# Low halves of split weights: by an accumulating DMA from GpSimd in place of a VectorE subtraction

## The chip, the cores and the metric

The kernel runs on one core of a Trainium2 chip, as one program in one launch. The metric is the device time of the whole program in microseconds (us). PE is TensorE, DVE VectorE, ACT ScalarE, POOL GpSimd, and SP is SyncE, which only issues DMAs here.

## The reference

One inference step of a two-layer encoder for two groups of tokens that share weights: 512 prompt positions and 32 later ones, 544 columns in all. For each layer, all in float32:

```
z = x @ w_in                                  # columns for three branches
A = chunked gMLP gating;  B = latent attention (8 heads);  C = RG-LRU
x = LN(ALPHA * x + concat(A, B, C) @ w_o)     # 1024 x 1024
up = x @ ffn_w_up                             # 1024 x 5632
f = gelu(conv3(up)[:, :2816]) * conv3(up)[:, 2816:]
x = LN(ALPHA * x + f @ ffn_w_down)            # 2816 x 1024
```

The outputs are x of both groups and a set of caches and states.

## The kernel before

Activations lie transposed, features on the 128 partitions and the 544 columns in the free dimension, in two halves of 272. To get more than the precision of one pass, each float32 operand a is split into a high part, rounded to the type float32r, and a low part a - high, also float32r. A product of two operands is then three matmuls (`mm3`, lines 89 to 91): high by high, high weight by low x, low weight by high x. TensorE runs nothing but such triples in the projections.

A weight tile is 128 partitions by up to 8 blocks of 128 columns (512 KB, or 448 KB with 7 blocks). `load_w` has SyncE load it into one of 4 raw buffers (`wr`). `split_w` takes a high and a low buffer (`wh`, `wl`, five of each, in rotation) and calls `split`: ScalarE copies the raw tile to the high part (line 64), VectorE subtracts the high part from the raw tile (line 67). `page_weights` does the same with two half tiles in general pages, for weights that are prepared well ahead of their stage. `gate` holds two instructions behind which the planner has to put the splits.

The order on each engine is made by a planner. It goes by program order as a priority, but moves what is ready in its own model ahead of what is not. Each engine then runs its queue strictly in order and waits by semaphores.

The stages of a layer that concern the change:

- `wo_stage`: eight tiles of w_o by `proj_ln`, with the sums for the LayerNorm between them. It also prepares the first five tiles of the up projection (`pre_up`: two in wh/wl buffers, three in pages).
- `ffn`: the 22 pairs (gate g and value v) of the up projection in three blocks of 7, 7 and 8, each followed by its share of the down projection (8 tiles of 7, 7 and 8 blocks; `proj` twice, `proj_ln` in the end). A plain tile (`up_w`) is 16 triples for each half. The pairs 8, 10, ..., 20 are mixed pairs instead: `forms` makes seven combinations of weights, `seven` multiplies them with combinations of x (A11, A12, then S2, S1, S3, then S4, A22), and its three parts run between the halves of the plain pair that follows:

```
fa, fb, fc, fd = pair(8), pair(8), pair(8), pair(4)   # four of the five wh and wl buffers
...
w = up_w(l, *tl)
for hv in range(2):
    ev(tl, hv, mms([w], KU, hv)[0])
    if mix is not None and next(mix, True):
```

- `ev` lets ScalarE copy a half out of PSUM into a page `xp`, whose first two columns GpSimd sets to zero (`begin`, line 1086), and `post` lets VectorE do the convolution.
- `pre_in` prepares three tiles of the next layer's w_in, two of them by `page_weights`.

The weights of the mixed pairs, of the mixers (`col_weights`, `weights`) and of w_in tile 0 keep the VectorE subtraction.

Of the kernel before, what the change touches and what calls it, by code (L numbers as in the profile page):

```python
# [8 lines left out]
F32R = mybir.dt.float32r  # L9
AF = mybir.ActivationFunctionType  # L10
ALU = mybir.AluOpType
# [13 lines left out]
NI = 22  # L25
# [21 lines left out]
def trunk_kernel(ctx: ExitStack, tc: tile.TileContext, i, o, k):  # L47
    nc = tc.nc
    pool = ctx.enter_context(tc.tile_pool(name="sb", bufs=1))
    psum = ctx.enter_context(tc.tile_pool(name="ps", bufs=1, space=bass.MemoryType.PSUM))  # L50
    dram = ctx.enter_context(tc.tile_pool(name="dr", bufs=1, space=bass.MemoryType.DRAM))
    BUFS = dict(pg=28, pt=12, kb=8, pp=6, wr=4, wh=5, wl=5)

    def page(name, dt=F32, tag="pg"):
        return pool.tile([128, W if tag == "pp" else PG], dt, tag=tag, name=name, bufs=BUFS[tag])
# [7 lines left out]
    def act(out, in_, func=AF.Copy, **kw):  # L63
        return nc.scalar.activation(out=out, in_=in_, func=func, **kw)  # L64

    def tt(out, a, b, op, e=None):
        return (e or nc.vector).tensor_tensor(out=out, in0=a, in1=b, op=op)  # L67

    def stt(out, a, s, b, op0, op1):
        return nc.vector.scalar_tensor_tensor(out=out, in0=a, scalar=s, in1=b, op0=op0, op1=op1)  # L70
# [7 lines left out]
    def split(hi, lo, src, e=None):  # L78
        act(hi, src)
        tt(lo, src, hi.bitcast(F32), ALU.subtract, e)  # L80
# [12 lines left out]
    gate = []  # L93
    def load_w(src, kk, cols, name):
        wr = pool.tile([128, kk, cols], F32, tag="wr", name=name + "r", bufs=BUFS["wr"])
        nc.sync.dma_start(out=wr, in_=src)
        return wr
# [4 lines left out]
    def split_w(wr, kk, cols, name):  # L102
        wh = pool.tile([128, kk, cols], F32R, tag="wh", name=name + "h", bufs=BUFS["wh"])
        wl = pool.tile([128, kk, cols], F32R, tag="wl", name=name + "l", bufs=BUFS["wl"])
        with ExitStack() as st:
            for ins in gate:
                st.enter_context(tc.issue_after(ins.ins))
            split(wh, wl, wr)
        return wh, wl

    def weights(src, kk, cols, name):
        return split_w(load_w(src, kk, cols, name), kk, cols, name)

    def rsqrt(y, v, t):
        a = act(y, v, AF.Abs_reciprocal_sqrt)
        tt(t, y, y, ALU.mult)
        stt(t, t, -0.5, v, ALU.mult, ALU.mult)
        return a, stt(y, t, 1.5, y, ALU.add, ALU.mult)
# [84 lines left out]
    def col_weights(src, kk, name, kper=8):  # L203
        res = []
        for c in range(0, kk, kper):
            n = min(kper, kk - c)
            wh, wl = weights(src[:, 128 * c:128 * (c + n)].rearrange("p (k c) -> p k c", k=n), n, 128, name)
            for j in range(n):
                res.append((wh, wl, j))
        return res  # L210

    def page_weights(src, name, tag="pg"):
        wr = load_w(src.rearrange("p (k c) -> p k c", k=8), 8, 128, name)
        res = []
        for c in (0, 4):
            h, lo = page(name + "h", F32R, tag), page(name + "l", F32R, tag)
            h, lo = (t[:, 0:512].rearrange("p (k c) -> p k c", k=4) for t in (h, lo))
            with ExitStack() as st:
                for ins in gate:
                    st.enter_context(tc.issue_after(ins.ins))  # L220
                split(h, lo, wr[:, c:c + 4, :])
            res += [(h, lo, j) for j in range(4)]
        return res

    def mms(ws, kts, hv, hook=None, at=2):
        bs = [bank("mm") for _ in ws]
        nk = len(kts)
        for j in range(nk):
            for b, w in zip(bs, ws):
                wh, wl, ci = w[j]  # L230
                rh, rl = kts[j]
                mm3(b[:, 0:HW], wh[:, ci, :], wl[:, ci, :], rh[:, HV[hv]], rl[:, HV[hv]], j == 0, j == nk - 1)
            if hook is not None and j == at:
                hook()
        return [b[:, 0:HW] for b in bs]
# [707 lines left out]
            if self.spill is not None:  # L943
                nc.sync.dma_start(out=self.spill[m], in_=x)

    def proj(wsrc, kts, evac, name, kper):
        for ms in ((0, 1), (2,), (3,), (4,), (5,), (6,), (7,)):
            ws = [col_weights(wsrc(m), len(kts), f"{name}{m}", kper) for m in ms]
            for hv in range(2):
                for m, ps in zip(ms, mms(ws, kts, hv)):  # L950
                    evac(m, hv, ps)

    def proj_ln(wsrc, kts, ln, name, kper, ns, pre, mid, ko=None):
        n1 = 8 - ns

        def get(m):
            w = col_weights(wsrc(m), len(kts), f"{name}{m}", kper)
            return [w[j] for j in ko] if ko else w

        for ms in ((0, 1), (2,), (3,)):  # L960
            ws = [get(m) for m in ms]
            for hv in range(2):
                for m, ps in zip(ms, mms(ws, kts, hv)):
                    ln.evac(m, hv, ps)
            if ms[0] == 0 and mid is not None:
                mid()
        w = get(4)
        for hv in range(2):
            ps = mms([w], kts, hv)[0]
            ln.shift(hv)  # L970
            ln.evac(4, hv, ps)
        for m in range(5, n1):
            w = get(m)
            for hv in range(2):
                ln.evac(m, hv, mms([w], kts, hv)[0])
        ln.warm()
        ws = [get(m) for m in range(n1, 8)]
        nxt = pre() if pre is not None else None
        for j in range(ns):
            ln.evac(n1 + j, 0, mms([ws[j]], kts, 0)[0])  # L980
        for j in range(ns):
            ps = mms([ws[j]], kts, 1, (lambda: ln.stats(0)) if j == 0 else None, 5)[0]
            if j == 0 and not ln.final:
                ln.apply(0, range(4))
            ln.evac(n1 + j, 1, ps)
        if ln.final:
            ln.stats(1)
            ln.apply(0)
        else:
            ln.apply(0, range(4, 8))  # L990

        def hook():
            if not ln.final:
                ln.stats(1)
            ln.apply(1)
        rest = [] if ln.final else [lambda m=m: ln.settle(m) for m in range(8)]
        return nxt, hook, rest

    def wo_stage(l, va, pre):
        xT = []  # L1000
        for m in range(8):
            x = page(f"xT{m}")
            nc.sync.dma_start(out=x[:, 0:W], in_=xd[l][m])
            if m >= 4:
                act(x[:, 0:W], x[:, 0:W], scale=ALPHA)
            xT.append(x)
        ln = LN(xT, "alpha", va, C_LN1G, C_LN1B, None, False)
        ko = [6, 7, 2, 3, 0, 4, 1, 5]

        kts = [KX[m] for m in ko]  # L1010
        return xT, *proj_ln(lambda m: i["wo"][l, m], kts, ln, "wo", 8, 3, pre, None, ko)

    def up_w(l, i_, s):
        return col_weights(i["wup"][l, NI * s + i_], 8, "wup", 8)

    def pre_up(l):
        return [up_w(l, j // 2, j % 2) if j < 2 else page_weights(i["wup"][l, NI * (j % 2) + j // 2], "wup") for j in range(5)]
# [45 lines left out]
    def ffn(l, va, vf, xT, first, hook, rest, pre):  # L1063
# [13 lines left out]
        for bl, (i0, nk) in enumerate(BLK):  # L1077
            fts = []
# [84 lines left out]
            for tl in tiles[done:]:  # L1163
# [6 lines left out]
                w = up_w(l, *tl)  # L1170
# [5 lines left out]
            def wsrc(m):  # L1176
                return i["wdn"][l, m, :, 128 * i0:128 * (i0 + nk)]

            if bl < len(BLK) - 1:
                def ev2(m, hv, ps):  # L1180
                    x = xT[m][:, HV[hv]]
                    if bl == 0:
                        stt(x, x, ALPHA, ps, ALU.mult, ALU.add)
                    else:
                        tt(x, x, ps, ALU.add)
                proj(wsrc, fts, ev2, "wd", 8)
            else:
                fin = l == DEPTH - 1

                def mid():  # L1190
                    nc.sync.dma_start(out=o[7][l], in_=fo)

                ln = LN(xT, "add", va, C_LN2G, C_LN2B, o[0] if fin else xd[l + 1], fin)
                nxt = proj_ln(wsrc, fts, ln, "wd", 8, 2, pre, mid)
        return nxt

    def pre_in(l):
        res = []
        for m in range(3):
            w = col_weights if m == 0 else page_weights  # L1200
            res.append(w(i["win"][l, m], 8, f"win{m}") if m == 0 else w(i["win"][l, m], f"win{m}"))
        return res

    vecs = {}
    nxt, hook = load_x()
    rest = []
    for l in range(DEPTH):
        mixer(l, nxt, hook, rest)
        va, vf, kvg, sp4 = vecs[l]
        xT, nxt, hook, rest = wo_stage(l, va, lambda: pre_up(l))  # L1210
        nxt, hook, rest = ffn(l, va, vf, xT, nxt, hook, rest, (lambda: pre_in(l + 1)) if l + 1 < DEPTH else None)
# [119 lines left out]
```

## Time and profile before

| | |
|---|---|
| median of 3 runs | 1272.6 us (1271.58 to 1275.66) |
| profiled execution, its own time | 1273.21 us |
| its span, first to last instruction | 1271.2 us |
| granted TensorE clock, mean | 0.996 of full speed |
| busy: TensorE matmul / weight load | 1247.2 us / 1202.8 us |
| busy: VectorE / ScalarE / GpSimd | 920.4 us / 710.3 us / 48.4 us |
| moved by DMA | 124.59 MB, 98 GB/s on average |

The span is what the instructions of the profiled execution cover; its own time has some 2 us around it. Busy times are the union of an engine's instructions. Matmuls overlap in their records (288 ns each at a pace of one in about 126 ns), so small gaps between them don't show in the busy time.

### The profile page before, as it was taken

How to read it: one execution, taken by the hardware profiler on the slowest of the kernel's cores; microseconds unless marked ns; L12 is line 12 of the kernel's file. 1: busy time of each engine (PE TensorE's matmuls, PEld its weight loads, DVE VectorE, ACT ScalarE, POOL GpSimd, SP SyncE). 2: the span in 40 equal slices, each digit the busy share in tenths (PEclk: the TensorE clock that was granted, in tenths of full speed). 3: DMA queues.
4: the chain of work that ended last, by engine and by line, in shares of the span. 5: the costliest groups of instructions: out<-in, count | busy, mean ns of one | idle time of the engine just before them, and what ended most of it. 6: DMA issues, size and time to landing. Idle time of an engine off the chain costs nothing.

```text
span 1271.2 us, 24212 instructions
## 1 busy us (share of the span) xinstructions
PE 1247.2 (98%) x9514; PEld 1202.8 (95%) x9514; DVE 920.4 (72%) x1885; ACT 710.3 (56%) x1533; POOL 48.4 (4%) x222
## 2 busy tenths in 40 slices
PE   8999999999999999999999999999999999999995
PEld 8999879999999999999999997899999999999994
DVE  6766877996456855877886767699964587467867
ACT  6475764596236724664465767447852475156723
POOL 2500000000000000000000100000000000000000
PEclk9999999999999999999999999999999999999998
DMA  9243434033212422424143433331322223231402
GB/s 297 82 120 90 122 128 133 18 101 86 97 67 84 117 67 68 131 85 147 31 153 108 128 97 90 139 107 51 92 76 84 67 90 111 84 100 67 136 1 71
DMA packets 49170, 124.59 MB, mean 98 GB/s; under 512 B 7577, under 2 KB 15257, under 8 KB 49057
## 3 DMA queue, kind: packets, MB, share of 16 engines
q1 hardware_dynamic: 49056, 123.06, 30.9%
q8 instruction: 74, 1.21, 0.4%
q14 instruction: 40, 0.32, 0.1%
HBM read 112.61 MB, written 5.97 MB: 93 GB/s over the span
## 4 chain that ended last, share of the span: by engine, by line
PE 87%; DVE 7%; ACT 3%; DMA 1%; issue 1%; DVEq 0%; ACTq 0%
PE mm L89 24%; PE mm L90 24%; PE mm L91 23%; DVE xT L70 2%; PE ov L244 1%; DVE ac L70 1%; PE pT L133 1%; PE ol L244 1%; PE s L89 1%; PE kv L389 1%; PE kv L390 1%; PE kv L388 1%; PE s L90 1%; PE s L91 1%; DVE xT L67 1%
## 5 line engine op out<-in xcount | busy, mean ns | idle before, releaser
L90 PE MATMUL mm<-xl,wuph 128*128 128x272 f32 x960 | 276.4, 288 | 0.0
L91 PE MATMUL mm<-xh,wupl 128*128 128x272 f32 x960 | 276.2, 288 | 0.0
L89 PE MATMUL mm<-xh,wuph 128*128 128x272 f32 x960 | 275.1, 289 | 0.9 <-DVE xT L67 0.9
L89 PEld LDWEIGHTS mm<-xh,wuph 128*128 128x128 f32 x960 | 180.1, 188 | 1.6 <-DVE xT L67 1.3
L90 PEld LDWEIGHTS mm<-xl,wuph 128*128 128x128 f32 x960 | 180.6, 188 | 0.2
L91 PEld LDWEIGHTS mm<-xh,wupl 128*128 128x128 f32 x960 | 180.6, 188 | 0.0
L70 DVE SCALAR_TENSOR_TENSOR ac<-xp,vf,ac 128x544 f32<-128x544 f32 x176 | 134.3, 779 | 1.7
L64 ACT ACTIVATE wfwh<-wupr 128x1024 fp32r<-128x1024 f32 (+1 forms) x56 | 53.2, 950 | 94.8 <-PE mm L90 87.0
L64 ACT ACTIVATE wuph<-wupr 128x1024 fp32r<-128x1024 f32 (+1 forms) x66 | 64.0, 981 | 57.4 <-PE mm L90 48.6
L64 ACT ACTIVATE xp<-mm 128x272 f32<-128x272 f32 x162 | 62.9, 389 | 43.7 <-PE mm L91 43.5
L67 DVE TENSOR_TENSOR wupl<-wupr,wuph 128x1024 fp32r<-128x1024 f32 (+1 forms) x66 | 73.6, 1123 | 15.0 <-ACT wuph L64 15.0
L67 DVE TENSOR_TENSOR wfwl<-wupr,wfwh 128x1024 fp32r<-128x1024 f32 (+1 forms) x56 | 61.0, 1089 | 32.2 <-ACT wfwh L64 31.8
L67 DVE TENSOR_TENSOR xT<-xT,mm 128x272 f32<-128x272 f32 x80 | 33.7, 434 | 50.9 <-PE mm L91 50.8
L64 ACT ACTIVATE ac<-mm,vf 128x272 f32<-128x272 f32 x120 | 69.0, 575 | 0.0
L89 PE MATMUL mm<-th,wfwh 128*128 128x272 f32 x224 | 65.6, 297 | 0.0
L91 PE MATMUL mm<-th,wfwl 128*128 128x272 f32 x224 | 64.1, 288 | 0.0
L90 PE MATMUL mm<-tl,wfwh 128*128 128x272 f32 x224 | 64.1, 288 | 0.0
L70 DVE SCALAR_TENSOR_TENSOR xT<-xT,mm 128x272 f32<-128x272 f32 x48 | 20.6, 437 | 50.0 <-PE mm L91 49.7
L91 PE MATMUL mm<-xh,wfwl 128*128 128x272 f32 x168 | 48.5, 289 | 0.0
L90 PE MATMUL mm<-xl,wfwh 128*128 128x272 f32 x168 | 48.5, 289 | 0.0
L89 PE MATMUL mm<-xh,wfwh 128*128 128x272 f32 x168 | 48.3, 288 | 0.0
L64 ACT ACTIVATE fh<-ac 128x544 fp32r<-128x544 f32 x44 | 28.9, 657 | 30.8 <-DVE ac L67 30.5
(516 smaller groups left out, 3976.4 us busy)
## 6 DMA issues: line engine op xcount, KB each, us to landing
wupr<-in_wup_dram SPq DMA_DIRECT2D x88, 512.0 KB
xT<-in_x_dram SPq DMA_DIRECT2D x16, 136.0 KB
xT<-in_x_dram SPq DMA_DIRECT2D x8, 272.0 KB
xd<-xT SPq DMA_DIRECT2D x8, 272.0 KB
xT<-xd SPq DMA_DIRECT2D x8, 272.0 KB
out_dram<-xT SPq DMA_DIRECT2D x16, 136.0 KB
ckT<-in_ckT_dram SPq DMA_DIRECT2D x8, 256.0 KB
cr<-in_ck_dram SPq DMA_DIRECT2D x8, 256.0 KB
```

Source lines behind the costliest of these rows:

```text
L64: return nc.scalar.activation(out=out, in_=in_, func=func, **kw)
L67: return (e or nc.vector).tensor_tensor(out=out, in0=a, in1=b, op=op)
L70: return nc.vector.scalar_tensor_tensor(out=out, in0=a, scalar=s, in1=b, op0=op0, op1=op1)
L89: nc.tensor.matmul(ps, lh, rh, start=start, stop=False, **kw)
L90: nc.tensor.matmul(ps, lh, rl, start=False, stop=False, **kw)
L91: lastmm[0] = nc.tensor.matmul(ps, ll, rh, start=False, stop=stop, **kw)
L133: nc.tensor.transpose(out, in_, ident[0:p, 0:p])
L244: nc.tensor.matmul(ps, a, b, start=start, stop=stop)
L388: nc.tensor.matmul(b[0:n, 0:288], XH[j][:, cs], wh[:, ci, :], start=j == 0, stop=False)
L389: nc.tensor.matmul(b[0:n, 0:288], XL[j][:, cs], wh[:, ci, :], start=False, stop=False)
L390: nc.tensor.matmul(b[0:n, 0:288], XH[j][:, cs], wl[:, ci, :], start=False, stop=j == 7)
```

## The change

`lo_by_dma` makes the low part: ScalarE writes the high part and then a second, negated copy of the raw tile, rounded to float32r as well, into the low buffer. GpSimd then issues a DMA that reads the same float32 weights from HBM again and adds them onto the negated copy. VectorE has no part in it. `unit_weights` (w_o, the plain tiles of the up projection, the down projection) and `page_weights` use it.

```diff
+    def lo_by_dma(wh, wl, wr, src):
+        with ExitStack() as st:
+            for ins in gate:
+                st.enter_context(tc.issue_after(ins.ins))
+            act(wh, wr)
+            act(wl, wr, scale=-1.0)
+        nc.gpsimd.dma_start(out=wl, in_=src, accum_op=ALU.add)
+        return wh, wl
+
+    def unit_weights(src, kk, name):
+        src = src.rearrange("p (k c) -> p k c", k=kk)
+        wr = load_w(src, kk, 128, name)
+        wh = pool.tile([128, kk, 128], F32R, tag="wh", name=name + "h", bufs=BUFS["wh"])
+        wl = pool.tile([128, kk, 128], F32R, tag="wl", name=name + "l", bufs=BUFS["wl"])
+        lo_by_dma(wh, wl, wr, src)
+        return [(wh, wl, j) for j in range(kk)]
...
     def page_weights(src, name, tag="pg"):
-        wr = load_w(src.rearrange("p (k c) -> p k c", k=8), 8, 128, name)
+        src = src.rearrange("p (k c) -> p k c", k=8)
+        wr = load_w(src, 8, 128, name)
...
-            with ExitStack() as st:
-                for ins in gate:
-                    st.enter_context(tc.issue_after(ins.ins))
-                split(h, lo, wr[:, c:c + 4, :])
+            lo_by_dma(h, lo, wr[:, c:c + 4, :], src[:, c:c + 4, :])
...
-    def proj(wsrc, kts, evac, name, kper):
+    def proj(wsrc, kts, evac, name):
...
-            ws = [col_weights(wsrc(m), len(kts), f"{name}{m}", kper) for m in ms]
+            ws = [unit_weights(wsrc(m), len(kts), f"{name}{m}") for m in ms]
...
-            w = col_weights(wsrc(m), len(kts), f"{name}{m}", kper)
+            w = unit_weights(wsrc(m), len(kts), f"{name}{m}")
...
     def up_w(l, i_, s):
-        return col_weights(i["wup"][l, NI * s + i_], 8, "wup", 8)
+        return unit_weights(i["wup"][l, NI * s + i_], 8, "wup")
```

## Rows read from the trace of the kernel before

**Rows 1.** Page, part 1: busy us (share of the span) x instructions.
```profile
PE 1247.2 (98%) x9514; PEld 1202.8 (95%) x9514; DVE 920.4 (72%) x1885; ACT 710.3 (56%) x1533; POOL 48.4 (4%) x222
```
**Rows 2.** Waits of TensorE: us in total, times, longest us.
```profile
PE mm L89 <- ACT xh L64: 5.7, 2, 4.1
PE ln L891 <- DVE lns L67: 2.4, 2, 1.8
```
**Rows 3.** Waits in the first 20 us.
```profile
PE mm L89 <- ACT xh L64: 4.1, 1, 4.1
```
**Rows 4.** Instructions on the up projection's split tiles: ns min/median/max, first, last start.
```profile
L67 DVE TENSOR_TENSOR wupl<-wupr,wuph x66: 682/1218/1227, 204.3 to 1184.5; 128x1024 fp32r<-128x1024 f32 x54, 128x512 fp32r<-128x512 f32 x12
...
L64 ACT ACTIVATE wuph<-wupr x66: 614/1060/1087, 203.7 to 1183.2; 128x1024 fp32r<-128x1024 f32 x54, 128x512 fp32r<-128x512 f32 x12
```
**Rows 5.** Windows: length, busy PE, PEld, DVE, ACT, POOL, clock, DMA share, GB/s.
```profile
254.00:352.00 98.00, 97.80 (x779) 97.58 (x779) 68.48 (x110) 58.60 (x124) 1.31 (x13) 1.00 0.31 97
...
260.00:280.00 20.00, 20.00 (x162) 20.00 (x161) 20.00 (x39) 19.97 (x48) 0.40 (x4) 1.00 0.29 101
...
377.90:380.90 3.00, 3.00 (x26) 3.00 (x26) 2.90 (x6) 2.00 (x3) 0.10 (x1) 1.00 0.53 175
```
**Rows 6.** Page, part 3: packets, MB, share of 16 DMA engines' span.
```profile
q1 hardware_dynamic: 49056, 123.06, 30.9%
```
**Rows 7.** Timeline of TensorE, one mixed pair's first part to the second plain tile.
```profile
374.83 0.29 PE L89 MATMUL mm<-xh,wfwh 128*128 128x272 f32 x1
...
377.85 0.29 PE L89 MATMUL mm<-xh,wuph 128*128 128x272 f32 x1
...
378.10 0.29 PE L91 MATMUL mm<-xh,wupl 128*128 128x272 f32 x1
...
380.87 0.29 PE L89 MATMUL mm<-th,wfwh 128*128 128x272 f32 x1
...
391.65 0.29 PE L91 MATMUL mm<-xh,wupl 128*128 128x272 f32 x1
```
**Rows 8.** Timeline of SyncE's queue, a load of 512 KB.
```profile
183.77 0.33 SPq L96 DMA_DIRECT2D wo4r<-in_wo_dram  x1
```
**Rows 9.** Timeline of ScalarE, the split that waits for that load.
```profile
186.95 1.06 ACT L64 ACTIVATE wo4h<-wo4r 128x1024 fp32r<-128x1024 f32 x1 [1.72 <-DMA wo4r<-in_wo_dram]
```
**Rows 10.** Chain that ended last, 826 to 836 us: start, us, what.
```profile
829.70 5.72 DMA wupr<-in_wup_dram
```
**Rows 11.** Instructions on tile k: SyncE's slowest kind of issue.
```profile
L526 SPq DMA_DIRECT2D k<-krT x16: 742/760/827, 94.3 to 785.1; - x16
```
**Rows 12.** Timeline of ScalarE, the same tile of two down projections.
```profile
302.22 0.95 ACT L64 ACTIVATE wd1h<-wd1r 128x896 fp32r<-128x896 f32 x1 [0.63 <-PE mm L90]
...
434.47 0.95 ACT L64 ACTIVATE wd1h<-wd1r 128x896 fp32r<-128x896 f32 x1 [1.71 <-PE mm L90]
```
**Rows 13.** Timeline of TensorE, first use of the low parts of those two.
```profile
320.82 0.29 PE L91 MATMUL mm<-fh,wd1l 128*128 128x272 f32 x1
...
444.06 0.29 PE L91 MATMUL mm<-fh,wd1l 128*128 128x272 f32 x1
```
**Rows 14.** Timeline of ScalarE, splits of plain tiles that follow a mixed pair's start.
```profile
374.90 1.06 ACT L64 ACTIVATE wuph<-wupr 128x1024 fp32r<-128x1024 f32 x1 [1.23 <-PE mm L90]
...
377.92 1.06 ACT L64 ACTIVATE wuph<-wupr 128x1024 fp32r<-128x1024 f32 x1 [0.87 <-PE mm L90]
...
1180.15 1.07 ACT L64 ACTIVATE wuph<-wupr 128x1024 fp32r<-128x1024 f32 x1
```
**Rows 15.** Timeline of VectorE, the low part of the first of them.
```profile
375.99 1.23 DVE L67 TENSOR_TENSOR wupl<-wupr,wuph 128x1024 fp32r<-128x1024 f32 x1 [3.01 <-ACT wuph L64]
```
**Rows 16.** Timeline of TensorE where the low part of x is late.
```profile
240.51 0.87 PE L89 MATMUL mm<-xh,wuph 128*128 128x272 f32 x4
241.22 0.28 PE L90 MATMUL mm<-xl,wuph 128*128 128x272 f32 x1
241.34 0.29 PE L91 MATMUL mm<-xh,wupl 128*128 128x272 f32 x1
```
**Rows 17.** Waits of GpSimd: us in total, times, longest us.
```profile
POOL xp L1086 <- DVE ac L70: 266.3, 28, 55.8
```

More of the change, by code (lines that the diff above doesn't have):

```diff
@@ L951, in proj, with proj_ln @@
                     evac(m, hv, ps)
-    def proj_ln(wsrc, kts, ln, name, kper, ns, pre, mid, ko=None):
+    def proj_ln(wsrc, kts, ln, name, ns, pre, mid, ko=None):
         n1 = 8 - ns
         def get(m):
-            w = col_weights(wsrc(m), len(kts), f"{name}{m}", kper)
+            w = unit_weights(wsrc(m), len(kts), f"{name}{m}")
             return [w[j] for j in ko] if ko else w
@@ L1010, in wo_stage @@
         kts = [KX[m] for m in ko]
-        return xT, *proj_ln(lambda m: i["wo"][l, m], kts, ln, "wo", 8, 3, pre, None, ko)
+        return xT, *proj_ln(lambda m: i["wo"][l, m], kts, ln, "wo", 3, pre, None, ko)
     def up_w(l, i_, s):
-        return col_weights(i["wup"][l, NI * s + i_], 8, "wup", 8)
+        return unit_weights(i["wup"][l, NI * s + i_], 8, "wup")
     def pre_up(l):
@@ L1185, in ev2 @@
                         tt(x, x, ps, ALU.add)
-                proj(wsrc, fts, ev2, "wd", 8)
+                proj(wsrc, fts, ev2, "wd")
             else:
@@ L1193, in ffn @@
                 ln = LN(xT, "add", va, C_LN2G, C_LN2B, o[0] if fin else xd[l + 1], fin)
-                nxt = proj_ln(wsrc, fts, ln, "wd", 8, 2, pre, mid)
+                nxt = proj_ln(wsrc, fts, ln, "wd", 2, pre, mid)
         return nxt
```

## The prediction

> **What bounds the kernel now.** I read the page's busy times first, then the waits of TensorE, then the timelines of one stage. TensorE's matmuls cover 98% of the span, VectorE is busy 72% of it, ScalarE 56% and GpSimd 4% [rows 1]. TensorE almost never waits for anything: its two large waits are 5.7 and 2.4 us in total [rows 2], and 4.1 us of the first is one wait at the very start, before any changed weight is used [rows 3]. So at most about 5.7 - 4.1 + 2.4 = 4 us can be won by making VectorE faster, 0.3% of the span; the rest of what the change does can only be hidden or cost time. What decides is whether each low part, by its new and longer way, is still there when TensorE first reads it.
>
> **What is removed.** Where the change reaches, VectorE loses one subtraction per weight: 1.22 us for 128x1024 [rows 4]. In all 118 whole tiles (54 of the up projection, 16 of w_o, 48 of the down projection, of which 32 have 896 columns) and 16 half tiles (12 in these rows, 4 of win1 and win2), near 118 x 1.2 + 16 x 0.68 = 152 us of VectorE. VectorE is not what TensorE waits for, so this buys at most the 4 us above. The likely share is the LayerNorm stretches between projections, where VectorE is in TensorE's way; I take 1 us.
>
> **What is added on ScalarE.** A second pass per tile at the price of the first, 1.06 us [rows 4], near 134 us; ScalarE goes from 710 to some 845 us busy [rows 1]. In most stretches it has room. The tight one is 260 to 280 us, where it is busy 19.97 of 20 [rows 5]; three to four tiles are split there at one per 6.0 us, so some 4 us are pushed back; plain stretches have a long lead (below) that covers it, so I cost it at nothing. Without that cover TensorE would lose these 4 us once in each layer, 8 us.
>
> **What is added on the DMA queues and GpSimd.** Each whole tile is read from HBM a second time: 54 + 16 + 16 tiles of 512 KB, 32 of 448 KB and 16 of 256 KB, about 64 MB. The present 123.06 MB keep the 16 engines busy 30.9% of 1271.2 us, 393 us [rows 6], so 512 KB (0.524 MB) cost 1.67 us of all engines. An accumulating transfer is nowhere in this trace. From below it costs what a copy does, 1.67 us; from above, with the old value read and the sum written as two transfers of their own, 5.0 us. I take two, 3.35 us: the old low part has to be read as well as the weight, while a write goes beside reads in a copy too. Then the added load is 122 x 3.35 = 409 us and the engines go from 31% to 63% busy. In the first block of the FFN there are only plain tiles, one per 6.0 us (a half takes 377.85 to 380.87 [rows 7]), and the engines are 31% busy [rows 5]; a tile then needs 1.67 + 3.35 = 5.0 of 6.0 us. It fits, though not with much to spare.
>
> The Trainium skill (Collectives: The Full Stack, section "The bandwidth ceiling: the fold count and why AG ≠ RS ≠ AR") says that an add inside the DMA engine is slow not for its arithmetic but for its two source reads, which halve the rate. By it the price would be 3.35 us too and never 5.0; no row here can show that, and the sum keeps both bounds.
>
> **The latency of one low part.** Now: high part on ScalarE, then the subtraction. After: high part, negated high part, a wait of GpSimd, the issue, the transfer, its completion. Landing of one plain 512 KB load: SyncE issues at 183.77 [rows 8], ScalarE, which waits for it, starts at 186.95 [rows 9], so 3.2 us with little else in flight; among several loads the chain shows 5.72 us [rows 10]. For the accumulating one I bound 3.2 (a copy) to 6.4 us (two transfers one after the other) and take 3.2 + 1.67 = 4.9 us, plus half of the 2.5 us that other loads can add (5.72 - 3.2), because SyncE's loads fill half of the engines just then: 53% in 377.9 to 380.9 [rows 5]. The issue by GpSimd is not in the trace either; SyncE's takes 0.33 us [rows 8], its dearest kind 0.8 [rows 11], and I take 0.5. In sum 4.9 + 1.25 + 0.5 = 6.65 us behind the negated copy.
>
> The Trainium skill (DMA: Bandwidth & Descriptors, section "Latency and other measured facts") gives the first byte of a DMA issued from GpSimd as about 1 us against 0.6 us from SyncE. By it each low part would be 0.4 us later still, some 6 us over the fourteen places below; no run here shows it yet.
>
> **Where the longer way fits.** High and low parts rotate through five buffers each, and ScalarE fills one when TensorE leaves the tile five earlier. In plain stretches that is four tiles of lead: wd1 is split at 302.22 [rows 12] and read at 320.82 [rows 13], 18.6 us. A chain of 2 x 0.95 + 6.65 us hides in it. At the start of a down projection behind mixed tiles it is 9.6 us (434.47 to 444.06) [rows 12, 13]: 1.9 + 6.65 fits by a microsecond, and at the upper bound (1.9 + 0.5 + 6.4 + 2.5 = 11.3) it misses by 1.7 us, four times.
>
> **Where it does not fit.** A mixed pair (forms and seven) takes four of the five buffers. The first plain tile after it gets the buffer of the last plain tile before it, and between the two TensorE has only the products A11 and A12. In the trace: TensorE turns to them at 374.83 [rows 7], ScalarE starts the high part at 374.90 [rows 14], VectorE ends the low part at 375.99 + 1.23 = 377.22 [rows 15], and TensorE begins the tile at 377.85 and reads its low part at 378.10 [rows 7]. The slack is 0.88 us. The same pattern stands 14 times, seven to a layer, with splits from 374.90 to 1180.15. The second plain tile behind it is no problem: split at 377.92 [rows 14], read at 391.65 [rows 7].
>
> After the change the negated copy ends at about 374.90 + 1.06 + 1.06 = 377.0, and the low part is there at 377.0 + 6.65 = 383.7, or between 380.5 (0.33 + 3.2) and 386.7 (0.8 + 6.4 + 2.5). Against 378.10 that is 2.4 to 8.6 us late, 5.6 in the middle. But the order of TensorE is made by a planner that moves ready matmuls ahead: around 240.5 four L89 run before the first L90 and L91, because the low part of x was late [rows 16]. The 16 matmuls of this half that need only high parts can go first; only two of them stand before the first L91 now, so L91 can begin 14 x 0.126 = 1.8 us later at no loss (24 matmuls take 377.85 to 380.87 [rows 7]). Next in the program are the products S2, S1 and S3, 36 matmuls or 4.5 us; they could be moved too, if the planner's own idea of the transfer is long enough. I take the high parts as moved and of the products only three matmuls of S1: 5.6 - 1.8 - 0.4 = 3.4 us lost. Fourteen of them are 48 us. TensorE then waits with nothing behind it in its order, and the next tiles, ScalarE's evacuations and the releases move by as much, so it is not won back.
>
> GpSimd's queue is in order and also holds the memsets of xp, which wait for VectorE, 266 us in total over 28 of them and 55.8 us the longest [rows 17]. A transfer put behind such a memset waits with it, and a memset behind a transfer waits for ScalarE's copy, which waits for a buffer. Because both become ready in the order of the tiles, I cost this at nothing; a single bad place would cost up to some 10 us.
>
> **Sum.** The profiled execution took 1273.2 us (span 1271.2); the median of the runs is 1272.6, so it stands for them. 1273.2 - 1 + 48 = 1320 us, 3.7% slower.
>
> **Rivals.**
> *Hidden (not slower).* The planner also moves S1, S2 and S3 ahead of the tile. With their 4.5 us and the 1.8 us TensorE has work until 378.1 + 6.3 = 384.4, past the 383.7 of the middle estimate. For it: the moving shown in [rows 16]. Against it: S2 starts in a bank that VectorE must first read, and all depends on the planner expecting at least the real latency. It holds up to a chain of 384.4 - 374.9 = 9.5 us; then the time is 1270 to 1276.
> *Partly hidden.* 0.3 to 2 us at each place: 1277 to 1300.
> *Transfers become the bound.* If an accumulating 512 KB takes over 4.3 us of all engines, a plain tile needs more than its 6.0 us. At 6.7 us (four copies) the tiles of dense stretches (8 of w_o, 14 up and 24 down in a layer, 92) lose 2.4 us each, 220 us, and the 14 places 3.4 + 3.35 = 6.8 us each, 95 us: near 1590. At 5.0 us it is near 1273 + 92 x 0.67 + 14 x (3.4 + 1.65) = 1405. For it: nothing in the trace has the price. Against it: 31% of the engines' time is used now.
> *Faster.* VectorE's relief clears the LayerNorm stretches and all transfers hide: 1272.6 - 4 = 1268.6.
>
> **How the numbers follow.** A measurement here tells 0.3%, 3.8 us, from no change. Forecast (2 to 6 us at each of the 14, 1300 to 1357): 0.45. Hidden: 0.17. Partly hidden: 0.13. Transfers as the bound or slow (over 1357): 0.21. Faster: 0.04. So slower 0.79, same 0.17, faster 0.04. The range goes from 1271, which takes in nearly all of hidden, to 1400, which leaves about 0.12 of the slow end out. The forecast's own range is 1300 to 1357.
>
> **What would show it.** Right: TensorE gains waits at wupl, released by a DMA, seven to a layer and 2 to 6 us each, and none in the first FFN block; VectorE near 770 us busy and ScalarE near 845; transfers of GpSimd near 64 MB landing 5 to 8 us after the negated copy. Wrong: waits in plain stretches or at w_o (transfers are the bound), waits of TensorE for ScalarE or a late memset (order), or S products ahead of the tile and no wait (hidden).

## The result and the profile after

The changed kernel takes 1393.4 us (median of 4 runs, 1386.7 to 1398.8) against 1272.7 us: a ratio of 1.094 (95% interval 1.089 to 1.099), 120.7 us slower. 1320 us were forecast, 47 us slower than before. The sign, the 14 places and the wide range (1271 to 1400) held; the forecast's own range (1300 to 1357) did not, and the loss is two and a half times the forecast one.

The profiled execution took 1392.6 us with a span of 1390.8 us, 119.6 more than before. First the busy times, to be held against [rows 1]:

```profile
PE 1290.0 (93%) x9514; PEld 1239.5 (89%) x9514; DVE 790.0 (57%) x1751; ACT 816.2 (59%) x1667; POOL 169.0 (12%) x356
```

TensorE executes the same 9514 matmuls and is busy 42.8 us longer (1290.0 - 1247.2); the other 76.8 us of the 119.6 it stands empty. So there are two losses, waits and slower matmuls. The waits of TensorE, beside [rows 2]:

```profile
PE mm L91 <- DMA wupl<-in_wup_dram: 58.5, 14, 4.9
PE ln L906 <- DVE lns L67: 12.4, 3, 5.3
PE mm L91 <- DMA wd1l<-in_wdn_dram: 9.1, 4, 3.2
PE mm L89 <- ACT xh L64: 5.7, 2, 4.1
```

The 14 waits for a low part of the up projection are there, 4.18 us each. New beside them are four waits for wd1 in the later down projections; LayerNorm's waits grow from 2.4 us to 12.4. The timeline of one of the 14 places (ScalarE, GpSimd, TensorE), which answers to [rows 7, 14, 15]:

```profile
381.93 1.06 ACT L64 ACTIVATE wuph<-wupr 128x1024 fp32r<-128x1024 f32 x1 [1.23 <-PE mm L90]
...
383.73 1.06 ACT L64 ACTIVATE wupl<-wupr 128x1024 fp32r<-128x1024 f32 x1
...
385.19 0.86 POOL L120 DMA_DIRECT2D wupl<-in_wup_dram  x1 [27.61 <-PE mm L91]
...
384.87 0.29 PE L89 MATMUL mm<-xh,wuph 128*128 128x272 f32 x1
...
388.40 0.29 PE L89 MATMUL mm<-th,wfwh 128*128 128x272 f32 x1
392.74 0.39 PE L91 MATMUL mm<-xh,wupl 128*128 128x272 f32 x1 [4.05 <-DMA wupl<-in_wup_dram]
```

From the release of the buffer to the first use of the low part it is 392.74 - 381.93 = 10.8 us. TensorE begins the tile at 384.87, executes 27 matmuls that don't need the low part (22 of the products S1 to S3, L89 to L91 on th and tl, moved ahead, and 5 of the tile's own), and has nothing left at 388.7. The other places look the same: 17 to 22 of the products and 3 to 6 of the tile's own. The windows of the same place (length, busy PE, PEld, DVE, ACT, POOL, granted clock, DMA share, GB/s), and the stretch at the end of the output projection:

```profile
387.00:388.00 1.00, 1.00 (x8) 0.83 (x7) 0.75 (x2) 0.45 (x2) 0.36 (x1) 1.00 1.05 250
...
392.00:393.00 1.00, 0.26 (x2) 0.27 (x3) 0.00 (x0) 0.00 (x0) 0.00 (x0) 1.00 1.10 373
393.00:394.00 1.00, 1.00 (x8) 1.00 (x8) 0.00 (x0) 0.00 (x0) 0.00 (x0) 0.77 1.03 238
394.00:395.00 1.00, 1.00 (x7) 1.00 (x6) 0.00 (x0) 0.00 (x0) 0.00 (x0) 0.50 1.09 229
...
396.00:397.00 1.00, 1.00 (x6) 1.00 (x6) 0.00 (x0) 0.00 (x0) 0.00 (x0) 0.52 0.00 0
397.00:398.00 1.00, 1.00 (x11) 1.00 (x9) 0.00 (x0) 0.61 (x2) 0.00 (x0) 1.00 0.00 0
...
200.00:220.00 20.00, 20.00 (x158) 19.84 (x158) 4.55 (x12) 10.96 (x19) 6.11 (x7) 1.00 1.06 267
```

This is the second loss. After the wait the granted clock stands at 0.50, TensorE's lower level of 1.2 GHz instead of 2.4, and the matmuls come 0.226 us apart instead of 0.126. The drop goes with each of the 14 waits, and TensorE works some 3 to 6 us at the lower level; one more stands in each LayerNorm stretch behind an output projection and one at 690 us, at the border of the layers. Busy time weighted with the missing clock, added over windows of 1 us, gives 40.4 us (33.4 at the 14 places, 5.3 in the LayerNorm stretches, 1.7 at 690); in the kernel before the windows print 1.00 wherever TensorE is busy, so there it is 0 (its first microseconds are another matter; see the part on why the size was missed).

The transfers: packets, MB and share of 16 engines' span, and the issues with KB and us to landing, beside [rows 6]:

```profile
q1 hardware_dynamic: 49056, 123.06, 27.9%
q0 software_dynamic: 19296, 63.97, 25.5%
...
wupl<-in_wup_dram POOLq DMA_DIRECT2D x54, 512.0 KB, 7.8
```

An accumulating 512 KB lands 7.8 us after GpSimd turns to its issue (which takes it 0.86 us), and costs the engines 0.255 x 1390.8 / 122 = 2.91 us.

The LayerNorm stretch, on ScalarE's timeline:

```profile
217.31 0.63 ACT L64 ACTIVATE wuph<-wupr 128x512 fp32r<-128x512 f32 x1 [1.10 <-DMA wupr<-in_wup_dram]
217.97 0.40 ACT L64 ACTIVATE lnc<-lnm 128x272 f32<-128x272 f32 x1
```

LayerNorm's lnc stands in ScalarE's order behind the split of a tile of the next projection, and that split waits for its raw load. The DMA engines are full here (share 1.06 above), so I read the load as late for that, and with it lnc, VectorE's work and TensorE; experiments 5 and 7 try it.

### The profile page after: what moved, and what is told of

Same layout as the page of the kernel before. It is cut to its first block, busy times and chain, and to the rows that moved or that the text cites. A ratio compares the mean times of both kernels' runs of the same rounds, so it can differ in the third digit from the quotient of the medians.

```text
span 1390.8 us, 24420 instructions
## 1 busy us (share of the span) xinstructions
PE 1290.0 (93%) x9514; PEld 1239.5 (89%) x9514; DVE 790.0 (57%) x1751; ACT 816.2 (59%) x1667; POOL 169.0 (12%) x356
## 3 DMA queue, kind: packets, MB, share of 16 engines
q0 software_dynamic: 19296, 63.97, 25.5%
## 4 chain that ended last, share of the span: by engine, by line
PE 71%; DMA 15%; issue 6%; DVE 4%; ACT 4%; POOLq 0%; DVEq 0%; ACTq 0%
PE mm L91 19%; PE mm L89 19%; PE mm L90 19%; DMA wupl<-in_wup_dram 8%; DMA wd1l<-in_wdn_dram 2%; DMA wupr<-in_wup_dram 2%; PE ov L259 1%; DMA wd7l<-in_wdn_dram 1%; DVE xT L70 1%; DVE xT L67 1%; PE pT L150 1%; PE ol L259 1%; PE s L89 1%; PE kv L404 1%; PE kv L405 1%
## 5 line engine op out<-in xcount | busy, mean ns | idle before, releaser
L91 PE MATMUL mm<-xh,wupl 128*128 128x272 f32 x960 | 292.0, 305 | 58.5 <-DMA wupl<-in_wup_dram 58.5
L89 PE MATMUL mm<-xh,wuph 128*128 128x272 f32 x960 | 288.4, 302 | 0.2 <-ACT wuph L64 0.2
L91 PEld LDWEIGHTS mm<-xh,wupl 128*128 128x128 f32 x960 | 194.5, 203 | 61.7 <-DMA wupl<-in_wup_dram 61.6
L89 PEld LDWEIGHTS mm<-xh,wuph 128*128 128x128 f32 x960 | 193.3, 202 | 2.0 <-ACT wuph L64 1.6
L90 PEld LDWEIGHTS mm<-xl,wuph 128*128 128x128 f32 x960 | 193.0, 201 | 0.0
L67 DVE TENSOR_TENSOR xp<-xp,mm 128x272 f32<-128x272 f32 x28 | 12.2, 435 | 166.1 <-PE mm L91 158.4
L120 POOL DMA_DIRECT2D wupl<-in_wup_dram x66 | 57.6, 872 | 335.1 <-ACT wupl L64 159.8
L89 PE MATMUL mm<-th,wfwh 128*128 128x272 f32 x224 | 67.8, 303 | 0.2
L91 PE MATMUL mm<-th,wfwl 128*128 128x272 f32 x224 | 65.3, 291 | 0.0
L64 ACT ACTIVATE wupl<-wupr 128x1024 fp32r<-128x1024 f32 (+1 forms) x66 | 64.4, 976 | 0.0
L1101 POOL MEMSET xp<- 128x2 f32 x88 | 21.8, 297 | 257.9 <-DVE ac L70 186.5
L67 DVE TENSOR_TENSOR fl<-ac,fh 128x544 fp32r<-128x544 f32 x44 | 31.9, 725 | 33.5 <-ACT fh L64 33.5
```

The costliest lines, as they stand in the source:

```text
L89: nc.tensor.matmul(ps, lh, rh, start=start, stop=False, **kw)
L90: nc.tensor.matmul(ps, lh, rl, start=False, stop=False, **kw)
L91: lastmm[0] = nc.tensor.matmul(ps, ll, rh, start=False, stop=stop, **kw)
L120: nc.gpsimd.dma_start(out=wl, in_=src, accum_op=ALU.add)
L1101: nc.gpsimd.memset(xp[tl][:, 0:2], 0.0)
```

## The experiments

The theory: the 14 late low parts cost their waits, and each empty TensorE then costs a stretch at half clock. Rivals: the transfers, or ScalarE's second pass, slow the kernel or the clock in themselves; the low part's lateness comes from full DMA engines.

**1. The 14 tiles back on VectorE (e1_undo14).**

```diff
     def up_w(l, i_, s):
+        if s == 0 and i_ - 1 in SPL:
+            return col_weights(i["wup"][l, NI * s + i_], 8, "wup", 8)
         return unit_weights(i["wup"][l, NI * s + i_], 8, "wup")
```

> The changed kernel, but the low parts of the 14 tiles that follow a mixed pair are made by VectorE again; all other plain weights keep the accumulating DMA (about 90% of its transfers). Theory (these 14 late low parts cost their waits, 58.5 us, and the TensorE clock falls because of these waits, near 33 us at half pace): both go, 1393 - 58.5 - 33 = near 1300 us, granted clock 0.99, clock loss only in the two LayerNorm stretches. Rival (the clock falls because of the transfers or of ScalarE's second pass as such): only the waits go, near 1335 us, and the clock stays near 0.96. Rival (the load of the transfers slows the whole): the waits move to other places, over 1350 us.

Measured: 1286.9 us, ratio to before 1.0117 (1.0088 to 1.0146), granted clock 0.990. Waits of TensorE:

```profile
PE ln L906 <- DVE lns L67: 12.6, 3, 6.3
...
PE mm L91 <- DMA wd1l<-in_wdn_dram: 3.3, 4, 1.7
```

Giving back 14 of some 134 weights removes 106.5 of the 120.7 us, with 56.6 of the 64 MB still moved by the accumulating queue. Only the two LayerNorm stretches still show a drop (5.3 us). Both rivals miss: the clock does not fall for the transfers, and the waits did not move elsewhere. The time is 13 us below the expectation. The waits for wd1 fell as well, from 9.1 to 3.3 us, and they fall to 3.3 us in experiment 3 too, where all low parts come as in the changed kernel; so some 6 us of them came with the waits and drops at the 14 places, in a way that was not tried.

**2. Only these 14 by the accumulating DMA (e2_only14).** The kernel before, with the same condition the other way round.

```diff
     def up_w(l, i_, s):
+        if s == 0 and i_ - 1 in SPL:
+            return unit_weights(i["wup"][l, NI * s + i_], 8, "wup")
         return col_weights(i["wup"][l, NI * s + i_], 8, "wup", 8)
```

> The kernel before, with the accumulating DMA for the low parts of the 14 tiles behind a mixed pair alone (14 of some 134 weights). Theory (each is late by its own chain of copy, issue and transfer, whatever else is moved): 1273 + 58.5 + 33 = near 1365 us, 14 waits of TensorE of about 4.2 us for a DMA and a clock drop behind each. Rival (the chain is long because the other accumulating transfers fill the engines): the transfer lands near 5 us after its issue instead of 7.8, the waits fall to 1 to 1.5 us and no clock drop follows, near 1290 us.

Measured: 1368.0 us, ratio 1.0756 (1.0725 to 1.0788). Waits of TensorE, queue and landing:

```profile
PE mm L91 <- DMA wupl<-in_wup_dram: 56.1, 14, 4.6
```

```profile
q0 software_dynamic: 2016, 7.34, 3.1%
wupl<-in_wup_dram POOLq DMA_DIRECT2D x14, 512.0 KB, 7.5
```

The 14 do it alone: 14 waits of 4.0 us, 14 drops (31.4 us). The rival that the other accumulating transfers crowd the engines falls: with GpSimd's queue at 3.1% instead of 25.5% a transfer still takes 7.5 us. SyncE's loads are still there (the engines are 0.70 busy in 377 to 386 us, at the first of these waits); no run lets such a transfer land alone.

**3. The same lateness without an empty TensorE (e3_filler).** 64 matmuls into another bank stand between the first two matmuls of the tile and the first that reads the low part.

```diff
+    def fill(wh, rh, n):
+        b = bank("fill", "ss")
+        for q in range(n):
+            r = nc.tensor.matmul(b[:, 0:HW], wh, rh, start=q == 0, stop=q == n - 1)
+        return r
...
-                    ev(tl, hv, mms([w], KU, hv)[0])
+                    ev(tl, hv, mms([w], KU, hv, filler=64 if hv == 0 and tl[1] == 0 and tl[0] - 1 in SPL else 0)[0])
```

> The changed kernel with 64 more matmuls (8.1 us) into a bank of their own in each of the 14 places, ahead of the first matmul that reads the late low part; their result is read by nobody. The low part is as late as before, but TensorE has no empty time there. If the clock falls because TensorE stood empty: no drop at the 14 places, 1273 + 14 x 8.1 + 9 (wd1) + 17 (LayerNorm stretches) = near 1412 us, granted clock over 0.99. If it falls for anything else that the change brings: the 14 drops stay and cost some 33 us more, near 1445 us.

Measured: 1400.7 us, ratio 1.0997 (1.0981 to 1.1014), granted clock 0.991, with 14 x 64 more matmuls. TensorE's timeline at the first place and the windows (columns as above):

```profile
385.10 8.27 PE L243 MATMUL fill<-xh,wuph 128*128 128x272 f32 x64
393.20 0.29 PE L259 MATMUL mm<-xh,wupl 128*128 128x272 f32 x1
```

```profile
393.00:394.00 1.00, 1.00 (x10) 1.00 (x10) 0.00 (x0) 0.00 (x0) 0.00 (x0) 1.00 1.01 221
394.00:395.00 1.00, 1.00 (x11) 1.00 (x10) 0.00 (x0) 0.00 (x0) 0.00 (x0) 1.00 1.09 229
```

The low part is as late as before and the DMA engines as full, but the clock stays at 1.00 at all 14 places. So at these places an empty TensorE is needed for the drop.

**4. An empty TensorE without any added transfer (e10_pool14, e12_pool_four).** The kernel before, with the subtraction of the 14 tiles on GpSimd, once, and then four times over.

```diff
+                act(wh, wr)
+                for q in range(4):
+                    nc.gpsimd.tensor_tensor(out=wl, in0=wr, in1=wh.bitcast(F32), op=ALU.subtract)
```

> The kernel before, with the subtraction of the 14 tiles behind a mixed pair moved from VectorE to GpSimd; no added DMA and no second pass on ScalarE. No row has GpSimd at 128x1024; from 64x32 in 0.38 to 0.47 us against 128x2 in 0.29 to 0.34 us I estimate 3 to 6 us. Theory (the clock falls because TensorE stands empty, whatever keeps it waiting): at 5 us and more the waits are 2 to 4 us and the 14 drops come back with no DMA in it, near 1273 + 14 x (3 + 2.4) = 1350 us; at 3 us there are hardly waits and no drops, near 1280 us. Rival (a drop needs the added transfers): waits without drops, 1273 + 14 x 3 = 1315 us, clock 0.995.

> The kernel before, with the subtraction of the 14 tiles behind a mixed pair made by GpSimd, four times over (the same result each time), 4 x 2.43 us: the low part is ready near 7.9 us after TensorE begins the tile, as late as with the accumulating DMA, with no added transfer and no second pass on ScalarE. Theory (an empty TensorE is enough for the clock to fall): 14 waits of some 4 us and a stretch at half clock behind each, 1286 + 56 + 30 = near 1370 us, and up to 20 us more, as VectorE's 128x544 operations took 955 instead of 778 ns beside GpSimd's work. Rival (the drop needs the transfers as well): the waits with the granted clock at 1.00, near 1340 us.

Once: 1286.0 us, ratio 1.0098 (1.0083 to 1.0113). GpSimd's group, and TensorE's wait:

```profile
L1022 POOL TENSOR_TENSOR wupl<-wupr,wuph 128x1024 fp32r<-128x1024 f32 x14 | 34.0, 2431 | 208.4 <-ACT wuph L64 208.4
```

```profile
PE mm L91 <- POOL wupl L1022: 2.7, 10, 0.3
```

At 2.43 us it is hardly late, and none of the 14 places shows a drop; this run decides nothing on the clock. Four times: 1421.9 us, ratio 1.1168 (1.115 to 1.1186), above the estimate. Waits and windows:

```profile
PE mm L89 <- DVE xp L67: 84.4, 10, 8.5
PE mm L91 <- POOL xp L1097: 28.0, 4, 7.2
```

```profile
380.00:382.00 2.00, 0.00 (x1) 0.00 (x0) 2.00 (x1) 0.00 (x0) 1.92 (x2) 1.00 0.00 0
...
384.00:386.00 2.00, 0.00 (x0) 0.00 (x0) 2.00 (x3) 0.66 (x1) 1.92 (x2) 0.50 0.00 0
386.00:388.00 2.00, 0.93 (x4) 0.94 (x5) 2.00 (x1) 0.00 (x0) 1.08 (x3) 0.50 0.02 4
388.00:390.00 2.00, 2.00 (x11) 2.00 (x11) 0.73 (x2) 0.00 (x0) 0.00 (x0) 0.50 0.88 289
```

The waits are 8 us, twice what was meant: the four subtractions take 10.8 us, and at ten places TensorE waits for an operation of VectorE's (on xp), which stands behind VectorE's other work; that work takes up to 2.9 us an operation beside GpSimd (see the last section). But the point is made: with a DMA share of 0.00 at this place, and at most 0.03 during any of the 14 waits, the clock falls to 0.50 behind an empty TensorE at all 14, 36.0 us in sum. Both halves are shown for these places: no drop without the wait, and a drop without the transfer.

**5. What the landing is made of (e6_copy).**

```diff
-        nc.gpsimd.dma_start(out=wl, in_=src, accum_op=ALU.add)
+        nc.gpsimd.dma_start(out=wl, in_=src)
```

> The changed kernel with a plain copy of the weight by GpSimd's queue in place of the accumulating transfer: the add is left out, so the low parts hold the whole weight. Same copies on ScalarE, same issues, same bytes from HBM. Theory (the read of the old low part and the add make the transfer long): the landing falls from 7.8 to near 5 us, 512 KB cost the engines near 1.65 instead of 2.91 us, the 14 waits shrink from 4.2 to near 1.5 us and the clock drops behind them go: 1393 - 38 - 33 = near 1322 us. Rival (a transfer of GpSimd's queue takes 7 to 8 us whatever it does): landing and waits stay, 1390 us.

Measured: 1311.9 us, ratio 1.0304 (1.0274 to 1.0334).

```profile
q0 software_dynamic: 19296, 63.97, 14.0%
wupl<-in_wup_dram POOLq DMA_DIRECT2D x54, 512.0 KB, 5.0
```

```profile
PE mm L91 <- DMA wupl<-in_wup_dram: 22.8, 14, 2.6
...
PE ln L906 <- DVE lns L67: 4.6, 3, 2.2
```

The accumulation costs 2.8 us of each landing, and engine time of 2.91 against 0.140 x 1314.9 / 122 = 1.51 us, 1.9 times a copy. Waits of 1.6 us remain, and drops behind 4 of the 14. LayerNorm's waits fall from 12.4 to 4.6 us and its two drops are gone, though ScalarE makes the same second passes: so its loss comes mainly from the accumulating transfers, not from the passes.

**6. An earlier start: the negated copy first (e4_neg_first), a sixth buffer (e9_six).**

```diff
-            act(wh, wr)
             act(wl, wr, scale=-1.0)
+            act(wh, wr)
```

> The changed kernel with ScalarE's negated copy ahead of the high part. In the place at 382 to 393 us two evacuations stood between the high part and the negated copy; so the copy ends 1.8 us earlier. Theory (the wait is the end of a fixed chain): the 14 waits shrink from 4.2 to near 2.4 us, 25 us less; the four waits of 2.3 us at wd1 show no clock drop, so with waits of that size the drops may go too: near 1335 us if they go, near 1368 us if they stay. Rival (the landing is set by the load of the DMA engines, not by when the transfer is issued): waits of 4 us and 1390 us as they are.

Measured: 1391.9 us, as before the edit. But it did not try what it was meant to. ScalarE's timeline at the place:

```profile
383.19 1.06 ACT L64 ACTIVATE wuph<-wupr 128x1024 fp32r<-128x1024 f32 x1 [1.22 <-PE mm L90]
...
384.99 1.06 ACT L64 ACTIVATE wupl<-wupr 128x1024 fp32r<-128x1024 f32 x1
```

The planner put the high part first all the same, here with the evacuations between the two, and at all 14 places. The run says nothing on the rival.

```diff
-    BUFS = dict(pg=28, pt=12, kb=8, pp=6, wr=4, wh=5, wl=5)
+    BUFS = dict(pg=26, pt=12, kb=8, pp=6, wr=3, wh=6, wl=6)
```

> The changed kernel with six buffers instead of five for the high and for the low parts, paid for with one raw buffer (three instead of four) and two pages (26 instead of 28). A period of a mixed pair and two plain tiles takes six buffers, so the first plain tile gets that of the plain tile two before it, free some 6 us earlier. Theory (the low parts are late because their buffer comes free one tile ahead): a lead of 10.9 + 6 - 6.8 us covers the chain, the 14 waits fall under 1 us, the clock drops go, and the time is near that of the kernel where VectorE makes these 14, 1287 us, plus up to 10 us for fewer raw buffers and pages. Rival (ScalarE's order or the three raw buffers set when the chain starts): waits of 3 us and more stay, over 1360 us.

Measured: 1359.9 us, ratio 1.0683 (1.0657 to 1.0708). Waits, and ScalarE and TensorE at the first place:

```profile
PE mm L91 <- DMA wupl<-in_wup_dram: 30.2, 14, 2.9
...
PE mm L91 <- DMA wo1l<-in_wo_dram: 9.1, 2, 4.6
```

```profile
395.54 1.06 ACT L64 ACTIVATE wuph<-wupr 128x1024 fp32r<-128x1024 f32 x1 [2.03 <-issue]
...
404.46 0.29 PE L89 MATMUL mm<-xh,wuph 128*128 128x272 f32 x1
```

The buffer comes 8.9 us ahead of the tile instead of 2.9, as meant. Yet the 14 waits only halve: at none of the 14 places are products of S1 to S3 moved ahead now, and TensorE has 2 matmuls to do before the low part instead of 27 (3.4 us of work). That the planner expected the low part sooner would explain it, but is not shown. Half of the expectation failed for that. There are also waits elsewhere (wo1 and others) that the changed kernel does not have; which of the fewer buffers brings them was not tried.

**7. Where the transfers are free (e8_hidden, e11_wo_dve, e14_wo_dve_order, e13_mixed_only).** e8 adds to experiment 1 that VectorE makes wd0 and wd1 of the later down projections and the five tiles split ahead of LayerNorm; e11 and e14 also the output projection's weights (below, a part of e14's edit).

```diff
-            w = unit_weights(wsrc(m), len(kts), f"{name}{m}")
+            w = (col_weights(wsrc(m), len(kts), f"{name}{m}", 8) if name == "wo" or m < 2 else
+                 unit_weights(wsrc(m), len(kts), f"{name}{m}"))
```

> VectorE makes the low parts wherever the changed kernel waited for one: the 14 tiles, wd0 and wd1 of the later down projections, and the five tiles that are split at the end of the output projection. All others keep the accumulating DMA (some 100 of 134). Theory (only late low parts cost time; the transfers, the issues, ScalarE's second pass cost nothing in themselves): 1272.5 +- 3 us, TensorE's clock at 0.995. Rival (the added transfers and copies cost something everywhere): 1280 us or more.

> The kernel in which VectorE makes all low parts that TensorE had waited for (run before at 1280.6 us), with the sixteen weights of the output projection made by VectorE too; some 84 weights keep the accumulating DMA. In that kernel the raw loads at the end of the output projection landed at 207.36 instead of 203.67 us, among its GpSimd transfers, and the work of LayerNorm stood behind their splits: 11.2 us lost in the two stretches, while the mixed blocks ran 2.2 us a layer shorter than before. Theory: without the transfers of the output projection the 11.2 us are gone, 1280.6 - 11.2 = near 1269.4 us, faster than both kernels by 0.25%. Rival (the rest of the transfers delays the LayerNorm stretches or something else): 1273 us or more.

> As the kernel at 1269.5 us that leaves the output projection and all waiting places to VectorE, but with the blocks of the output projection's weights in their proper order (there they were multiplied in the order in which they are stored, which left the result different and the number of operations the same). Both theories of that run: the same time, 1269.5 +- 1.5 us, faster than the kernel before by 0.2 to 0.4%; if the order of these blocks matters to the stretch behind the output projection, up to 1275 us.

e8: 1280.6 us, ratio 1.0062 (1.0042 to 1.0081), so its theory fell. Nor does the time fit the *everywhere* of its rival: each layer's mixed blocks take 2.2 us less than in the kernel before, and the loss stands at LayerNorm. Its wait, ScalarE's first split of an up projection's tile, and the window:

```profile
PE ln L912 <- DVE lns L67: 10.1, 3, 4.2
```

```profile
207.36 1.15 ACT L64 ACTIVATE wuph<-wupr 128x512 fp32r<-128x512 f32 x2 [3.54 <-DMA wupr<-in_wup_dram]
```

```profile
200.00:220.00 20.00, 19.85 (x155) 19.47 (x155) 10.42 (x23) 9.30 (x16) 1.46 (x3) 1.00 0.89 258
```

The split that began at 203.7 us before [rows 4] begins at 207.36: the raw load shares the engines with the low parts of the output projection. Without those, e11 takes 1269.5 us (0.9961 to 0.9981; it multiplies the output projection's blocks in stored order), and e14, with the blocks in their own order, 1270.4 us (0.9968 to 0.9989). e14:

```profile
PE ln L912 <- DVE lns L67: 1.8, 1, 1.8
```

```profile
200.00:220.00 20.00, 20.00 (x159) 19.84 (x158) 15.85 (x35) 10.92 (x19) 0.00 (x0) 1.00 0.52 185
```

So what the change adds in the output projection was LayerNorm's loss. These two runs take away the transfers and ScalarE's second passes together; experiment 5, which keeps the passes, points to the transfers.

e13 is the kernel before with the accumulating DMA for 36 weights.

```diff
-                w = up_w(l, *tl)
+                w = up_w(l, *tl, bl > 0 and tl[1] == 1)
...
-                proj(wsrc, fts, ev2, "wd", 8)
+                proj(wsrc, fts, ev2, "wd", 8, bl > 0)
```

> The kernel before, with the accumulating DMA only in the blocks that hold mixed pairs, and there only for the second plain tile behind a pair and for the down projection's later tiles: 36 weights. Theory (only there VectorE is in TensorE's way, and these low parts have a lead of a tile and more): the gain of the mixed blocks, 2.2 us a layer, and nothing lost, near 1268 us. Rival (the gain seen there belongs to transfers moved elsewhere, or the remaining waits of these blocks are not VectorE's): 1272.5 us.

Measured: 1269.8 us, ratio 0.9974 (0.9964 to 0.9985). On its page:

```profile
PE 1242.8 (98%) x9514; PEld 1202.9 (95%) x9514; DVE 885.8 (70%) x1849; ACT 740.0 (58%) x1569; POOL 79.4 (6%) x258
```

From the first matmul of a layer's first mixed pair to the layer's end TensorE takes 1.7 us less than in the kernel before in layer 0 and 2.3 us less in layer 1. It waits no less, but is busy 4.4 us less for the same matmuls; why stays open. e13, e11 and e14 are 0.2 to 0.3% faster than the kernel before. That is less than the 0.3% that the prediction takes as the mark of a change, though each interval leaves out a ratio of 1.

## Why the forecast had the sign and missed the size

**The step that failed is the sum.** It had a single term of loss, 14 places by 3.4 us of waiting, and priced TensorE's work behind a wait at full pace. The runs showed a second price, the stretch at half clock behind an empty TensorE: 33.4 us at these places, 40.4 in all. Experiments 3 and 4 show it from both sides. The price could have been read beforehand, behind the wait of 4.1 us that the prediction set aside as the start [rows 3]. TensorE's timeline and windows in the kernel before:

```profile
5.33 0.43 PE L90 MATMUL mm<-xl,win0h 128*128 128x272 f32 x1
5.55 0.43 PE L91 MATMUL mm<-xh,win0l 128*128 128x272 f32 x1
```

```profile
7.00:8.00 1.00, 1.00 (x5) 1.00 (x6) 0.76 (x2) 0.83 (x3) 0.00 (x0) 1.00 0.96 325
```

The windows print a granted clock of 1.00 there, but until 8.4 us the matmuls come some 0.226 us apart and take 0.43 us each, the numbers of the half clock behind the 14 waits; then it is 0.126 us. So beside the granted clock, the pace of the matmuls has to be read.

That 1393 lies in the range of 1271 to 1400 is luck: its upper end was for slow transfers, not for a slow TensorE.

**The 14 places: right in mechanism, a little short.** 48 us forecast, 58.5 measured, and 56.1 where nothing else was changed (e2). Two errors nearly cancel at the place shown. The chain was taken as 8.8 us and is 10.8: ScalarE puts two evacuations between high part and negated copy (0.7 us), and issue and landing take 7.95 us behind the copy (383.73 + 1.06 to 392.74) instead of 6.65. Against that the planner moved 22 matmuls of S1 to S3 ahead, not three, though of the tile's own high parts only 5 instead of 16 stand before the wait: 27 matmuls, some 1.4 us more cover than forecast. It is the start of the *hidden* rival, which got 2.8 of the 4.5 us of these products and would have needed a chain of 9.5.

**The price of a transfer: right side, somewhat high.** 3.35 us of all engines forecast, 2.91 measured; the plain stretches have no waits, as forecast, and *transfers become the bound* falls as a whole. The Trainium skill (Collectives: The Full Stack, section "The bandwidth ceiling: the fold count and why AG ≠ RS ≠ AR") lays the price of an add, in a ring between cores, to its second source read, a factor of two; experiment 5 agrees with 1.9. GpSimd's later first byte, which the prediction took from the Trainium skill (DMA: Bandwidth & Descriptors, section "Latency and other measured facts"), found no test: no run times the same transfer from both queues under the same load.

**wd1 in the later down projections: costed at nothing, 9.1 us measured.** The upper bound named there was 1.7 us, four times; the four waits are 1.2 to 3.2 us. Without the waits and drops at the 14 places (experiments 1 and 3) they are 0.2 to 1.7 us, 3.3 in sum, inside that bound: "fits by a microsecond" was no cover for a chain that grew by two, and the rest went with the losses at the 14 places.

**LayerNorm: a gain of 1 us forecast, a loss of 15 measured** (waits 12.4 - 2.4 = 10, clock 5.3). VectorE was relieved as forecast, but this was read as VectorE's stretch alone. It is one where SyncE already loads half of the time (share 0.52 in e14, which has no added transfers there), and in which ScalarE's in-order queue holds LayerNorm behind splits that wait for loads.

**At nothing, and rightly:** ScalarE's second pass in the plain blocks, GpSimd's queue order. VectorE's 790 and ScalarE's 816 us were forecast near 770 and 845.

In sum 58.5 + 33.4 (places) + 9.1 (wd1) + 15.3 (LayerNorm) + 1.7 (the drop at 690) = 118 of the 119.6 us. The sum is good to some 7 us only: in experiment 1 the same terms give 10.2 + 5.3 + 3.3 = 18.8 us, and its span is 12.2 us longer than before (1283.4 against 1271.2), so gains like those of the mixed blocks stand against the losses.

## What to carry to other kernels

A wait on TensorE can cost more than its length: look at the granted clock in the windows behind it, and price a new stall of some microseconds with the half pace that follows (here 2.4 us on top of each 4.2). Taking work from an engine that bounds nothing is free only where its results have lead, so ask tile by tile when the buffer comes free and when the tile is first read; 14 of 134 weights made 106.5 of the 120.7 us. And before adding traffic, look for the stretches where loads already fill half of the engines and other work stands behind their landing.

## What the runs showed of the hardware

The drop to the lower clock followed all 14 waits of 3.0 to 4.9 us in the changed kernel, 6 of 14 waits of 1.0 to 2.9 us with six buffers, 4 of 14 of 0.9 to 2.6 us with plain copies, and none of the four of 1.2 to 3.2 us at wd1. So the length of the wait alone does not tell it in this range. At the border of the layers TensorE waits 1.62 us in the changed kernel (688.72) and in the kernel before (630.03), and only the changed kernel shows a drop behind it. A drop can also come without such a wait: in the kernel of experiment 5 the granted clock falls to 0.50 at 165 us, in attention, where TensorE's last waits were 0.3 and 0.2 us. The Trainium skill (Trainium Architecture — The Big Picture, section "What this means for kernel authors") has TensorE at 1.2 or 2.4 GHz by its recent activity; experiments 3 and 4 agree.

An accumulating transfer of 512 KB takes 7.5 us to land where GpSimd's queue has 14 of them (3.1%) and 7.8 where it has all (25.5%); the plain one from the same queue took 5.0 (14.0%). These are medians, with SyncE's loads beside them.

GpSimd subtracts 128x1024 in 2.43 us, where VectorE takes 1.22 [rows 4], and slows VectorE beside it. VectorE's 128x544 operations take 782 ns in the mean in the changed kernel, 915 ns with one subtraction at each of the 14 places and 1055 ns with four. The mean hides two kinds: in the last kernel 22 of 176, those beside a subtraction, take 2.9 us, the others 0.78. Their shortest, median and longest there, in ns:

```profile
L70 DVE SCALAR_TENSOR_TENSOR ac<-xp,vf,ac x176: 772/779/2946, 261.7 to 1356.8; 128x544 f32<-128x544 f32 x176
```
